# Modulation of the first tiles summed on TensorE in column groups, with TensorE in the program's order

## The chip, the cores and the metric

The kernel runs on one core of a Trainium2 chip. The metric is the device time of one execution in microseconds (us).

## What is computed

Two transformer blocks run one after the other on a sequence of 512 tokens with 1024 features, in float32. The first block has a mixer (a state-space scan beside chunked attention) and a gated feed-forward layer; the second has windowed attention beside an mLSTM, and a mixture of experts. The change touches only the beginning of the first block, where the norm of the input is scaled and shifted by six vectors that a small product of the conditioning vector c gives:

```python
c_act = jax.nn.silu(c)
mod = (c_act @ w_ada[l] + b_ada[l])[:, None, :]
sh_m, sc_m, g_m, sh_f, sc_f, g_f = jnp.split(mod, 6, axis=-1)
h = rmsnorm(x, norm_mix_w[l]) * (1 + sc_m) + sh_m
z, xbc, dt_raw, q, k, v = jnp.split(h @ w_in[l], IN_SPLITS, axis=-1)
```

Only sh_m and sc_m, the first 2048 columns of w_ada, are wanted here; the other four vectors are made later, beside other work.

## The kernel before

Everything is kept transposed: features lie on the 128 partitions, so x is eight tiles xT[:, k, :] of 128 features by 512 tokens. A float32 product is made of three products of a faster type: each operand is split into a high and a low part, and mm3 (lines 273 to 279) issues high x high, low weight x high, high weight x low.

The stage of the change (lines 487 to 574) works off the eight feature tiles k. For each, load(k) fetches 1 MB of w_ada (all 1024 rows for 256 columns: 128 of the shift and 128 of the scale) and 384 KB of w_in. ScalarE makes the high part of the weights (whigh), VectorE the low part (wlow). The 256 modulation values of tile k are sums over 1024 rows, eight blocks of 128: VectorE multiplies the first ND[k] blocks by cact and adds them up (ada0), TensorE adds the rest as products with one column, and a product with ones sums over the partitions (lines 551 and 552). VectorE adds the bias and makes the scale (b, lines 556 and 557), ScalarE applies both to the normed tile xn (h, line 559) and takes its high part hh (line 560), VectorE the low part hl (line 565). Then products(k) adds w0[k] x h into six PSUM tiles (first), eighteen products per tile. The stage begins with the norm: squares on ScalarE, their sum on VectorE (acc), column sums on TensorE (line 361), the root on GpSimd (line 371), and a broadcast by four products with diagonal matrices (lines 380 and 381). Products of zeros (warm, line 244) are issued at the start and once in between.

The order of each engine's instructions is set by a planner at build time, which goes by priority and its own times. Where ip(...) stands, an instruction is held behind the one traced just before it on its engine; most of the stage's VectorE and ScalarE instructions are so held. TensorE's are held by it only in the modulation (lines 551 and 552); the products stand where the planner puts them, and it may put products of the following qk tiles (tile_a, lines 277 to 279 with wh and wl) between them. Tiles of PSUM come from a pool of two (psd) and one of six (psm). The qk tiles take theirs from the pool of two, and so does the first of the six tiles of the stage. The eight DMA loads of xT, four constants, and the loads of w_ada and w_in are issued by the SP queue in this order.

Of the kernel before, what the change touches and what calls it, by code (L numbers as in the profile page):

```python
# [13 lines left out]
AF = mybir.ActivationFunctionType  # L14
ALU = mybir.AluOpType
AX = mybir.AxisListType
PSUM = bass.MemoryType.PSUM
P = 128
EPS = 1e-6
NW0, NW1 = 16, 14  # L20
WAIT = 6
NEG = -1e30

# [159 lines left out]
def _prog(ctx, tc, nc, I, out):  # L183
    PE, DVE, ACT, POOL, SP = nc.tensor, nc.vector, nc.scalar, nc.gpsimd, nc.sync
    pers = ctx.enter_context(tc.tile_pool(name="pers", bufs=1))
# [3 lines left out]
    sm = dense.enter_context(tc.tile_pool(name="sm", bufs=2, side="right", reuse_waits="tile"))  # L189
# [10 lines left out]
    def pt(pool, shape, tag, dt=F32, bufs=None):  # L200
        kw = {} if bufs is None else {"bufs": bufs}
        return pool.tile(shape, dt, tag=tag, name=nm(tag), **kw)
# [8 lines left out]
    def psd():  # L211
        return pt(pd, [P, 512], "d")

    def psm():
        return pt(pm, [P, 512], "m")

    def const(name, shape, pool=pers):
        t = pt(pool, shape, name)
        SP.dma_start(t, I[name])
        return t  # L220
# [4 lines left out]
    HB = hbs.enter_context(tc.tile_pool(name="hb", bufs=1))  # L225
# [4 lines left out]
    xps = ExitStack()  # L230
    XP = xps.enter_context(tc.tile_pool(name="xp", bufs=1, reuse_waits="tile"))
    xT = pt(XP, [P, 8, 512], "xT")
    for k in range(8):
        SP.dma_start(xT[:, k, :], I["xT"][:, k, :])
    ident, tri, strict, ones = (const(n, [P, P], p) for n, p in (("k_ident", pers), ("k_tri", HB), ("k_strict", HB), ("k_ones", sm)))


    zeros = pt(XP, [P, 256], "zeros")
# [2 lines left out]
    def warm(n, zeros=zeros):  # L241
        ps = psm()
        for _ in range(n):
            PE.matmul(ps[:, :256], lhsT=zeros[:, :P], rhs=zeros, start=True, stop=True)
# [8 lines left out]
    def col(name, j=0, n=1):  # L253
        o, _ = _COLS[name]
        if kept:
            return kept[0][:, o - _COLS["final_norm_w"][0] + j :][:, :n]
        return cols[:, o + j : o + j + n]
# [17 lines left out]
    def mm3(ps, w, x, first, last):  # L275
        (wh, wl), (xh, xl) = w, x
        PE.matmul(ps, lhsT=wh, rhs=xh, start=first, stop=False)  # L277
        PE.matmul(ps, lhsT=wl, rhs=xh, start=False, stop=False)  # L278
        PE.matmul(ps, lhsT=wh, rhs=xl, start=False, stop=last)  # L279
# [104 lines left out]
    def norm_cols(n, *parts, ts=range(4), pool=sm):  # L384
        ms = pt(pool, [P, 4], "ms")[:, : len(ts)]
        DVE.tensor_scalar(ms, colsum(*parts, ts=ts, pool=pool), 1.0 / n, EPS, op0=ALU.mult, op1=ALU.add)
        return rstd(ms, pool)
# [36 lines left out]
    cact = pt(pers, [P, 8], "cact")  # L424
# [42 lines left out]
    with xps:  # L467

        hh = pt(HB, [P, 8, 512], "hh", F32R)
        hl = pt(HB, [P, 8, 512], "hl", F32R)  # L470
        def norm_split(oh, ol, x, R, g, ks, hs=slice(0, 512)):
            for k in ks:
                t = pt(XW, [P, 512], "nt")[:, hs]
                DVE.tensor_tensor(t, x[:, k, hs], R, op=ALU.mult)
                ACT.activation(oh[:, k, hs], t, AF.Copy, scale=g[:, k : k + 1])  # L475
                DVE.scalar_tensor_tensor(ol[:, k, hs], t, g[:, k : k + 1], oh[:, k, hs].bitcast(F32), op0=ALU.mult, op1=ALU.subtract)

        def mod_norm(R, s, b, hh, hl, hs):
            for k in range(8):
                t = pt(XW, [P, 512], "nt")[:, hs]  # L480
                DVE.tensor_tensor(t, xT[:, k, hs], R, op=ALU.mult)
                h = pt(XW, [P, 512], "nh")[:, hs]
# [1 line left out]
                split(hh[:, k, hs], hl[:, k, hs], h)  # L484


        with tc.tile_pool(name="ada", bufs=1, reuse_waits="tile") as AD:
            acc = pt(sm, [P, 512], "acc", bufs=1)
            for k in range(8):
                sq = acc if k == 0 else pt(AD, [P, 512], "sq", bufs=3)  # L490
                ACT.activation(sq, xT[:, k, :], AF.Square)
                if k:
                    DVE.tensor_tensor(acc, acc, sq, op=ALU.add)
            first = [psd()] + [psm() for _ in range(5)]
            ip = tc.keep_in_program_order
            wbuf = [pt(HB, [P, 4096], n) for n in ("bh", "bl")]
            wa, w0, whs, wls, xns, accs = [], [], [], [], [], []

            def load(k):
                if k < 8:  # L500
                    wa.append(wbuf[k % 4 // 2][:, 2048 * (k % 2) : 2048 * (k % 2) + 2048])
                    SP.dma_start(wa[k], I["w_ada0"][k])
                    w0.append(pt(AD, [P, 768], "w0", bufs=3))
                    SP.dma_start(w0[k], I["w_x0"][k])

            def ada0(k, a, b):

                if k < 8:
                    if a == 0:
                        accs.append(pt(AD, [P, 256], "acc", bufs=3))  # L510
                        ip(DVE.tensor_scalar(accs[k], wa[k][:, :256], cact[:, 0:1], None, op0=ALU.mult))
                    for i in range(max(a, 1), b):
                        ip(DVE.scalar_tensor_tensor(accs[k], wa[k][:, 256 * i : 256 * i + 256], cact[:, i : i + 1], accs[k], op0=ALU.mult, op1=ALU.add))

            def whigh(k):
                if k < 8:
                    whs.append(pt(AD, [P, 768], "w0h", F32R, bufs=3))
                    ip(ACT.activation(whs[k], w0[k], AF.Copy))

            def wlow(k):  # L520
                if k < 8:
                    wls.append(pt(AD, [P, 768], "w0l", F32R, bufs=3))
                    ip(DVE.tensor_tensor(wls[k], w0[k], whs[k].bitcast(F32), op=ALU.subtract))

            def xnorm(k):
                if k < 8:
                    xns.append(pt(AD, [P, 512], "xn", bufs=3))
                    ip(DVE.tensor_tensor(xns[k], xT[:, k, :], R, op=ALU.mult))

            ND = (5, 5, 6, 7, 6, 6, 7, 6)  # L530
            load(0)
            load(1)
            r = norm_cols(1024, acc)
            warm(4)
            whigh(0)
            ada0(0, 0, 3)
            R = rowbc(r)
            ada0(0, 3, ND[0])
            xnorm(0)
            Rs = pt(AD, [P, 512], "R")  # L540
            ACT.activation(Rs, R, AF.Copy)
            R = Rs
            whigh(1)

            def modulated(k):
                load(k + 2)
                ps = psm()
                for j in range(2):
                    for i in range(ND[k], 8):
                        o = 256 * i + j * P  # L550
                        ip(PE.matmul(ps[:, j : j + 1], lhsT=wa[k][:, o : o + P], rhs=cact[:, i : i + 1], start=(i == ND[k]), stop=False))
                    ip(PE.matmul(ps[:, j : j + 1], lhsT=accs[k][:, j * P : (j + 1) * P], rhs=ones[:, 0:1], start=False, stop=True))
                n = 3 if k else ND[1]
                ada0(k + 1, 0, n)
                b = pt(AD, [P, 3], "b", bufs=2)
                ip(DVE.tensor_tensor(b[:, :2], ps[:, :2], col("b_ada", k, 9)[:, ::8], op=ALU.add))
                ip(DVE.scalar_tensor_tensor(b[:, 2:], b[:, 1:2], 1.0, col("norm_mix_w", k), op0=ALU.add, op1=ALU.mult))
                h = pt(XW, [P, 512], "nh")
                ip(ACT.activation(h, xns[k], AF.Identity, bias=b[:, 0:1], scale=b[:, 2:]))
                ip(ACT.activation(hh[:, k, :], h, AF.Copy))  # L560
                ada0(k + 1, n, ND[min(k + 1, 7)])
                if k == 0:
                    wlow(0)
                wlow(k + 1)
                ip(DVE.tensor_tensor(hl[:, k, :], h, hh[:, k, :].bitcast(F32), op=ALU.subtract))
                xnorm(k + 1)
                whigh(k + 2)

            def products(k, *_):
                w = whs[k], wls[k]  # L570
                for m, o in enumerate(first):
                    mm3(o, [t[:, m * P : (m + 1) * P] for t in w], (hh[:, k, :], hl[:, k, :]), k == 0, k == 7)

            _pipelined([(k,) for k in range(8)], modulated, products)


        y, w_out = _mix1(locals())
# [48 lines left out]
        with tc.tile_pool(name="ffn", bufs=2, reuse_waits="tile") as FF:  # L626
            x = (hh, hl)
            for part, (a, b) in enumerate(_PARTS):
                ah = pt(HB, [P, 8, 512], "hh", F32R)
                al = pt(HB, [P, 8, 512], "hl", F32R)  # L630
                for m in range(a, b):
                    y = []
                    for j in range(2):
                        ps = ups.pop(0) if ups else tile_a(I["w_up"][2 * m + j], x)
                        o = pt(FF, [P, 512], "cv%d" % j)
# [11 lines left out]
                for m in range(8 if part < 2 else 5):  # L647
                    ps = tile_a(dn(m), (ah, al), kt=b - a)
# [64 lines left out]
    o, _ = _COLS["final_norm_w"]  # L713
# [39 lines left out]
    ip = tc.keep_in_program_order  # L753
# [44 lines left out]
def _pipelined(steps, *parts):  # L798

    steps = [list(s) for s in steps]  # L800
    for t in range(len(steps) + len(parts) - 1):
        for j, f in enumerate(parts):
            if 0 <= t - j < len(steps):
                steps[t - j].append(f(*steps[t - j]))
# [907 lines left out]
```

## Time and profile before

| | |
|---|---|
| time, median of 3 runs | 1591.37 us (1588.38 to 1591.61) |
| profiled execution | 1588.89 us, of which span 1587.1 us |
| mean granted TensorE clock | 0.992 |
| TensorE products busy | 1550.4 us, 98% |
| VectorE busy | 850.4 us, 54% |
| ScalarE busy | 524.4 us, 33% |
| HBM read | 315.41 MB |

Times within the span are counted from its start. A busy share over the whole span says little here, since the stage of the change is the first 75 us; it has to be read by windows and by the timeline. In the rows PE is TensorE's products, PEld its weight loads, DVE is VectorE, ACT ScalarE, SPq the queue of SP. Names such as d and m are tiles of the two PSUM pools, w0h and w0l the two parts of the stage's weights, wh and wl those of the qk tiles. A float32 product counts as two instructions, one of the split type as one.

### The profile page before, as it was taken

What the parts mean: (1) busy time and instruction counts of PE and PEld (TensorE: products, weight loads), DVE (VectorE), ACT (ScalarE), POOL (GpSimd) and SP (SyncE); (2) the same over time, 40 slices, a digit from 0 to 9 for tenths busy, and PEclk for the clock granted to TensorE, in tenths of its full rate; (3) what the DMA queues carried; (4) which work ended last, traced back from release to release, by engine and by line L of the source; (5) the groups of instructions that cost most, each with busy time, mean ns of one, the idle gap of its engine ahead of it and who ended that gap; (6) DMA issues with size and microseconds to landing.
All of it is one profiled execution on the core that took longest, in us unless ns stands there. A gap on an engine that the chain in (4) does not pass through costs nothing.

```text
span 1587.1 us, 21111 instructions
## 1 busy us (share of the span) xinstructions
PE 1550.4 (98%) x8208; PEld 1106.1 (70%) x8208; DVE 850.4 (54%) x1679; ACT 524.4 (33%) x964; POOL 35.8 (2%) x33
## 2 busy tenths in 40 slices
PE   8999999999999999989999999999999999999997
PEld 7878857988888888978976688866535545545443
DVE  7777886674564466668467724454242332332333
ACT  4453375442442344443456722231101101101101
POOL 0002000000000000000101000000000000000000
PEclk8999999999999999999999999999999999999999
DMA  8365423333233234402201023497999999999992
GB/s 331 135 197 175 167 73 101 126 100 106 100 94 104 95 93 128 145 18 98 89 27 57 29 86 98 141 316 271 392 369 418 418 415 418 419 417 417 418 417 75
DMA packets 92598, 321.02 MB, mean 202 GB/s; under 512 B 10412, under 2 KB 13100, under 8 KB 91472
## 3 DMA queue, kind: packets, MB, share of 16 engines
q1 hardware_dynamic: 92496, 319.64, 54.1%
q8 instruction: 66, 1.08, 0.3%
q14 instruction: 36, 0.29, 0.1%
HBM read 315.41 MB, written 4.19 MB: 201 GB/s over the span
## 4 chain that ended last, share of the span: by engine, by line
PE 90%; DVE 5%; ACT 2%; DMA 1%; issue 1%; POOL 1%; SPq 0%; DVEq 0%; ACTq 0%
PE d L1522 21%; PE d L277 15%; PE d L278 15%; PE d L279 15%; PE m L1508 4%; PE m L1624 4%; PE m L277 1%; PE m L279 1%; PE m L278 1%; PE m L1219 1%; PE m L1204 1%; DMA wr<-w_ada 1%; PE m L1039 1%; POOL rstd L371 1%; ACT S L1317 1%
## 5 line engine op out<-in xcount | busy, mean ns | idle before, releaser
L1522 PE MATMUL d<-we,xg 128*64 128x512 f32 x1024 | 226.6, 595 | 0.0
L261 DVE TENSOR_TENSOR wl<-wr,wh 128x1024 fp32r<-128x1024 f32 (+1 forms) x148 | 178.1, 1206 | 79.7 <-ACT wh L260 79.1
L277 PE MATMUL d<-bh,wh 128*128 128x512 f32 (+1 forms) x544 | 210.3, 387 | 2.6 <-ACT bh L475 1.5
L279 PE MATMUL d<-bl,wh 128*128 128x512 f32 (+1 forms) x544 | 209.7, 385 | 0.0
L278 PE MATMUL d<-bh,wl 128*128 128x512 f32 (+1 forms) x544 | 209.6, 385 | 0.0
L260 ACT ACTIVATE wh<-wr 128x1024 fp32r<-128x1024 f32 (+1 forms) x148 | 154.0, 1044 | 147.5 <-PE d L279 120.2
L1522 PEld LDWEIGHTS d<-we,xg 128*64 128x64 f32 x1024 | 70.8, 137 | 134.4 <-issue 121.6
L277 PE MATMUL d<-hh,wh 128*128 128x512 f32 (+1 forms) x392 | 147.2, 376 | 0.7 <-ACT bh L845 0.7
L278 PE MATMUL d<-hh,wl 128*128 128x512 f32 (+1 forms) x392 | 145.9, 373 | 0.0
L279 PE MATMUL d<-hl,wh 128*128 128x512 f32 (+1 forms) x392 | 145.8, 373 | 0.0
L277 PEld LDWEIGHTS d<-bh,wh 128*128 128x128 f32 x544 | 102.4, 188 | 25.0 <-issue 2.2
L278 PEld LDWEIGHTS d<-bh,wl 128*128 128x128 f32 x544 | 102.4, 188 | 22.2 <-issue 2.6
L279 PEld LDWEIGHTS d<-bl,wh 128*128 128x128 f32 x544 | 102.6, 189 | 20.1 <-issue 0.5
L1522 PE MATMUL d<-we,aT 128*64 128x512 f32 x512 | 112.6, 592 | 0.7 <-ACT aT L1597 0.7
L1522 PEld LDWEIGHTS d<-we,aT 128*64 128x64 f32 x512 | 36.7, 137 | 73.5 <-issue 71.4
L1625 DVE TENSOR_TENSOR xt<-xt,m 128x512 f32<-128x512 f32 x120 | 73.8, 681 | 22.8 <-PE m L1624 22.8
L277 PEld LDWEIGHTS d<-hh,wh 128*128 128x128 f32 x392 | 73.8, 188 | 16.8 <-issue 2.3
L1608 ACT ACTIVATE yh<-d,ws 128x512 fp32r<-128x512 f32 x32 | 22.0, 688 | 185.2 <-PE d L1522 185.2
L279 PEld LDWEIGHTS d<-hl,wh 128*128 128x128 f32 x392 | 73.7, 188 | 13.7 <-issue 0.5
L278 PEld LDWEIGHTS d<-hh,wl 128*128 128x128 f32 x392 | 73.9, 188 | 12.5
L638 DVE SCALAR_TENSOR_TENSOR cv<-d,cols,cv 128x511 f32<-128x511 f32 x41 | 30.7, 749 | 77.3 <-ACT cv L637 77.3
L1597 ACT ACTIVATE aT<-m 128x512 f32<-128x512 f32 x16 | 9.6, 598 | 176.5 <-PE m L1595 176.5
(430 smaller groups left out, 2631.6 us busy)
## 6 DMA issues: line engine op xcount, KB each, us to landing
we<-w_eg SPq DMA_DIRECT2D x128, 512.0 KB, 9.9
we<-w_eu SPq DMA_DIRECT2D x128, 512.0 KB, 8.9
we<-w_ed SPq DMA_DIRECT2D x128, 512.0 KB, 9.9
wr<-w_up SPq DMA_DIRECT2D x44, 512.0 KB, 3.3
wr<-w_ada SPq DMA_DIRECT2D x32, 512.0 KB, 4.0
wr<-w_out SPq DMA_DIRECT2D x16, 512.0 KB, 3.5
wr<-w_dn SPq DMA_DIRECT2D x16, 512.0 KB, 3.6
wr<-w_mg SPq DMA_DIRECT2D x16, 512.0 KB, 3.3
```

The lines of the kernel that those rows point to most:

```text
L260: ACT.activation(hi, src, AF.Copy)
L261: DVE.tensor_tensor(lo, src, hi.bitcast(F32), op=ALU.subtract)
L277: PE.matmul(ps, lhsT=wh, rhs=xh, start=first, stop=False)
L278: PE.matmul(ps, lhsT=wl, rhs=xh, start=False, stop=False)
L279: PE.matmul(ps, lhsT=wh, rhs=xl, start=False, stop=last)
L371: POOL.tensor_tensor(r, ms, mhalf.to_broadcast((P, n)), op=ALU.pow)
L638: DVE.scalar_tensor_tensor(o[:, 1:], ps[:, :511], wc(1), o[:, 1:], op0=ALU.mult, op1=ALU.add)
L1508: PE.matmul(ps[:, :n], lhsT=hx[:, T, d * P : (d + 1) * P], rhs=oh[:, T, :n], start=(T == 0 and hx is hth), stop=(T == 3 and hx is htl))
L1522: PE.matmul(ps[x * m : (x + 1) * m], lhsT=xs[x][:, k, :], rhs=w[k // 2][x][:, k % 2 * 512 : k % 2 * 512 + 512], start=(k == 0), stop=(k == ...
L1608: ACT.activation(yh[:, s], ps, AF.Copy, scale=ws)
L1624: PE.matmul(ps, lhsT=oht[:, T * P : (T + 1) * P], rhs=y[:, s], start=(i == 0), stop=(i == len(mm) - 1))
L1625: DVE.tensor_tensor(xt[:, T, s], xt[:, T, s] if len(done) > 1 else hth[:, T, s].bitcast(F32), ps, op=ALU.add)
```

## The change

VectorE's sums (ada0) and the one-column products are removed. Instead cact is laid out in a zeroed tile cz, 32 columns for each of the eight row blocks, of which the first holds the values. modulation(k) multiplies block i by the 256 columns of w_ada, in the column group i % 4 of 32 output partitions; the blocks i and i + 4 share a group. Each group then holds one row of partial sums and 31 of zeros. ScalarE copies the 128 x 256 result to SBUF (part), and columns(k) sums it over the partitions with two products with ones; b follows as before. modulation(k + 2) and whigh(k + 2) stand in the middle of products(k), columns(k + 1) ahead of products(k), and modulation(0) ahead of the norm's column sums. TensorE issues the whole block in the program's order. Besides, the opening products of zeros are 21 in place of 16, those in between 3 in place of 4, xT is loaded by four DMAs in place of eight, and two constants are loaded behind the first two tiles' weights.

```diff
-NW0, NW1 = 16, 14
+NW0, NW1, NW2 = 21, 14, 3
...
-    for k in range(8):
-        SP.dma_start(xT[:, k, :], I["xT"][:, k, :])
-    ident, tri, strict, ones = (const(n, [P, P], p) for n, p in (("k_ident", pers), ("k_tri", HB), ("k_strict", HB), ("k_ones", sm)))
+    for k in range(0, 8, 2):
+        SP.dma_start(xT[:, k : k + 2, :], I["xT"][:, k : k + 2, :])
+    ident, ones = (const(n, [P, P], p) for n, p in (("k_ident", pers), ("k_ones", sm)))
...
-        with tc.tile_pool(name="ada", bufs=1, reuse_waits="tile") as AD:
+        with tc.tile_pool(name="ada", bufs=1, reuse_waits="tile") as AD, tc.manual_schedule(engines={mybir.EngineType.PE}):
...
-            first = [psd()] + [psm() for _ in range(5)]
...
+            cz = pt(AD, [P, 8, 32], "cz")
+            DVE.memset(cz, 0.0)
+            DVE.tensor_copy(cz[:, :, 0], cact)
...
-            def ada0(k, a, b):
-
-                if k < 8:
-                    if a == 0:
-                        accs.append(pt(AD, [P, 256], "acc", bufs=3))
-                        ip(DVE.tensor_scalar(accs[k], wa[k][:, :256], cact[:, 0:1], None, op0=ALU.mult))
-                    for i in range(max(a, 1), b):
-                        ip(DVE.scalar_tensor_tensor(accs[k], wa[k][:, 256 * i : 256 * i + 256], cact[:, i : i + 1], accs[k], op0=ALU.mult, op1=ALU.add))
...
+            def modulation(k):
+
+                if k >= 8:
+                    return
+                ps = psm() if k % 2 else psd()
+                for i in range(8):
+                    g = 32 * (i % 4)
+                    PE.matmul(ps[g : g + 32, :256], lhsT=cz[:, i, :], rhs=wa[k][:, 256 * i : 256 * i + 256], start=(i < 4), stop=(i >= 4))
+                part = pt(AD, [P, 256], "acc", bufs=2)
+                mps.append((ps, part))
+                ip(ACT.activation(part, ps[:, :256], AF.Copy))
+
+            def columns(k):
+                if k >= 8:
+                    return
+                ps, part = mps[k]
+                for j in range(2):
+                    PE.matmul(ps[:, 256 + j : 257 + j], lhsT=part[:, j * P : (j + 1) * P], rhs=ones[:, 0:1], start=True, stop=True)
+                b = pt(AD, [P, 3], "b", bufs=3)
+                ip(DVE.tensor_tensor(b[:, :2], ps[:, 256:258], col("b_ada", k, 9)[:, ::8], op=ALU.add))
+                ip(DVE.scalar_tensor_tensor(b[:, 2:], b[:, 1:2], 1.0, col("norm_mix_w", k), op0=ALU.add, op1=ALU.mult))
+                bs.append(b)
+
             load(0)
             load(1)
+            tri, strict = (const(n, [P, P], HB) for n in ("k_tri", "k_strict"))
+            modulation(0)
             r = norm_cols(1024, acc)
-            warm(4)
+            columns(0)
+            warm(NW2)
             whigh(0)
-            ada0(0, 0, 3)
             R = rowbc(r)
-            ada0(0, 3, ND[0])
+            wlow(0)
             xnorm(0)
             Rs = pt(AD, [P, 512], "R")
             ACT.activation(Rs, R, AF.Copy)
             R = Rs
+            modulation(1)
             whigh(1)
+            first = [psd()] + [psm() for _ in range(5)]
...
             def modulated(k):
                 load(k + 2)
...
+                b = bs[k]
                 h = pt(XW, [P, 512], "nh")
                 ip(ACT.activation(h, xns[k], AF.Identity, bias=b[:, 0:1], scale=b[:, 2:]))
                 ip(ACT.activation(hh[:, k, :], h, AF.Copy))
-                ada0(k + 1, n, ND[min(k + 1, 7)])
-                if k == 0:
-                    wlow(0)
+                columns(k + 1)
                 wlow(k + 1)
                 ip(DVE.tensor_tensor(hl[:, k, :], h, hh[:, k, :].bitcast(F32), op=ALU.subtract))
                 xnorm(k + 1)
-                whigh(k + 2)
...
-            def products(k, *_):
+            def products(k):
                 w = whs[k], wls[k]
                 for m, o in enumerate(first):
                     mm3(o, [t[:, m * P : (m + 1) * P] for t in w], (hh[:, k, :], hl[:, k, :]), k == 0, k == 7)
+                    if m == 2:
+                        modulation(k + 2)
+                        whigh(k + 2)
...
-            _pipelined([(k,) for k in range(8)], modulated, products)
+            for k in range(8):
+                modulated(k)
+                products(k)
```

## Rows read from the trace of the kernel before

**Rows 1.** The page: the chain that ended last, its shares by engine.
```profile
PE 90%; DVE 5%; ACT 2%; DMA 1%; issue 1%; POOL 1%; SPq 0%; DVEq 0%; ACTq 0%
```

**Rows 2.** Windows: length, busy us (instructions) of PE, PEld, DVE, ACT, POOL; clock, DMA, GB/s.
```profile
30.00:35.00 5.00, 5.00 (x30) 4.32 (x29) 4.72 (x12) 2.29 (x3) 0.00 (x0) 1.00 0.94 358
```

**Rows 3.** Timeline of TensorE in the stage: start us, us, engine, line, operation, operands.
```profile
24.14 0.77 PE L277 MATMUL d<-hh,w0h 128*128 128x512 f32 x1
...
31.43 0.48 PE L277 MATMUL d<-hh,w0h 128*128 128x512 f32 x1
...
33.13 0.40 PE L279 MATMUL d<-hl,w0h 128*128 128x512 f32 x1
...
51.82 0.48 PE L277 MATMUL d<-hh,w0h 128*128 128x512 f32 x1
...
56.75 0.40 PE L277 MATMUL d<-hh,wh 128*128 128x512 f32 x1
...
70.55 0.40 PE L277 MATMUL d<-hh,wh 128*128 128x512 f32 x1
...
72.77 0.50 PE L277 MATMUL d<-hh,wh 128*128 128x512 f32 x1 [0.69 <-ACT bh L845]
```

**Rows 4.** Chain in order of time, 94 to 99 us, around narrow(): start us, us.
```profile
94.82 3.57 PE d L298 x32
98.39 0.43 PE d L277
98.82 0.23 PE d L278
```

**Rows 5.** Chain in order of time: two pieces of the one-column products.
```profile
46.37 0.34 PE m L551 x4
46.93 0.45 PE m L551 x4
```

**Rows 6.** Timeline of VectorE and ScalarE in one tile.
```profile
31.60 0.16 DVE L556 TENSOR_TENSOR b<-m,cols 128x2 f32<-128x2 f32 x1
31.80 0.16 DVE L557 SCALAR_TENSOR_TENSOR b<-b,cols 128x1 f32<-128x1 f32 x1
...
31.99 0.81 ACT L559 ACTIVATE nh<-xn,b 128x512 f32<-128x512 f32 x1 [0.78 <-DVE b L557]
...
32.84 0.63 ACT L560 ACTIVATE hh<-nh 128x512 fp32r<-128x512 f32 x1
...
33.83 0.95 DVE L523 TENSOR_TENSOR w0l<-w,w0h 128x768 fp32r<-128x768 f32 x1
...
34.70 0.68 DVE L565 TENSOR_TENSOR hl<-nh,hh 128x512 fp32r<-128x512 f32 x1
...
35.87 0.85 ACT L518 ACTIVATE w0h<-w 128x768 fp32r<-128x768 f32 x1 [2.39 <-PE m L279]
```

**Rows 7.** Timeline of the start.
```profile
1.22 8.60 PE L244 MATMUL m<-zeros 128*128 128x256 f32 x32 [1.22 <-DVE zeros L239]
...
9.10 0.33 SPq L502 DMA_DIRECT2D bh<-w_ada  x1
...
13.38 1.05 PE L361 MATMUL m<-k_ones,acc 128*128 128x1 f32 x8 [3.56 <-DVE acc L493]
...
15.76 0.88 DVE L380 TENSOR_SCALAR diag<-k_ident,rstd 128x128 f32<-128x128 f32 x4 [1.13 <-POOL rstd L371]
...
17.78 1.06 PE L381 MATMUL m<-diag,k_ones 128*128 128x128 f32 x8
```

**Rows 8.** Waits of TensorE: us in total, times, longest.
```profile
PE d L279 <- DVE wl L261: 2.7, 1, 2.7
```

**Rows 9.** DMA issues between 8 and 10 us: KB each, us to landing.
```profile
bh<-w_ada SPq DMA_DIRECT2D x1, 1024.0 KB, 5.4
```

**Rows 10.** Windows of TensorE alone: length, busy (instructions), clock, DMA, GB/s.
```profile
662.90:666.30 3.40, 2.54 (x23) 1.00 0.67 230
666.30:669.70 3.40, 3.40 (x18) 0.50 0.40 140
```

More of the change, by code (lines that the diff above doesn't have):

```diff
@@ L493, in _prog @@
                     DVE.tensor_tensor(acc, acc, sq, op=ALU.add)
-            first = [psd()] + [psm() for _ in range(5)]
             ip = tc.keep_in_program_order
             wbuf = [pt(HB, [P, 4096], n) for n in ("bh", "bl")]
-            wa, w0, whs, wls, xns, accs = [], [], [], [], [], []
+            wa, w0, whs, wls, xns = [], [], [], [], []
+            cz = pt(AD, [P, 8, 32], "cz")
+            DVE.memset(cz, 0.0)
+            DVE.tensor_copy(cz[:, :, 0], cact)
             def load(k):
@@ L528, in xnorm @@
                     ip(DVE.tensor_tensor(xns[k], xT[:, k, :], R, op=ALU.mult))
-            ND = (5, 5, 6, 7, 6, 6, 7, 6)
+            bs, mps = [], []
+            def modulation(k):
[18 more added lines that the diff above has]
+                bs.append(b)
             load(0)
             load(1)
+            tri, strict = (const(n, [P, P], HB) for n in ("k_tri", "k_strict"))
+            modulation(0)
             r = norm_cols(1024, acc)
-            warm(4)
+            columns(0)
+            warm(NW2)
             whigh(0)
-            ada0(0, 0, 3)
             R = rowbc(r)
-            ada0(0, 3, ND[0])
+            wlow(0)
             xnorm(0)
@@ L542, in _prog @@
             R = Rs
+            modulation(1)
             whigh(1)
+            first = [psd()] + [psm() for _ in range(5)]
             def modulated(k):
                 load(k + 2)
[L547 to L557, printed above, removed]
+                b = bs[k]
                 h = pt(XW, [P, 512], "nh")
```

## The prediction

> **What bounds the kernel now.** I read the page's shares of the chain first: TensorE carries 90% of what ended last [rows 1], so a stage costs what TensorE spends in it, waits included. The table by windows comes next: between 30 and 35 us, inside the stage that is rewritten, TensorE is busy 5.00 of 5 us and VectorE 4.72 [rows 2]; both are full, so relieving VectorE alone frees nothing unless TensorE also has less to do. Then TensorE's timeline [rows 3]. The stage's first product starts at 24.14. Tile 5 (I call the eight contraction blocks k tiles) starts at 51.82, products of the first qk tile come in between from 56.75, and from 70.55 the rest of that qk tile follows. The second qk tile starts at 72.77, after 0.69 us of waiting for a PSUM buffer. That start is my mark: all behind it is untouched code, so the change is worth what it does to these 72.77 us.
>
> **What is removed.** VectorE loses five to seven operations per tile (ada0). TensorE loses the one-column products of modulated(): pieces of four cost 0.34 to 0.45 us on the chain [rows 5], so the 12 to 16 instructions of most tiles cost 1.0 to 1.6 us, and they lay on TensorE's path.
>
> **What modulation(k) costs.** Eight products in four column groups are 16 instructions of 256 columns. The nearest rows are those of narrow(), the same form at 512 columns: 32 instructions in 3.57 us [rows 4], so half the count at half the width is 3.57 / 4 = 0.89 us if the groups overlap as there. The first full-width product behind it took 0.43 in place of 0.23 [rows 4], so going back costs 0.20; with the entry I take 1.2. The lower bound is 0.9; the upper, without overlap, is 16 x 0.27 = 4.3 by the opening warming products of the same width (8.60 us for 32) [rows 7]. I stay near the narrow rows. columns(k) is four one-column instructions, 0.34 to 0.45 [rows 5]; I take 0.5 with the switch.
>
> **What the order costs, the term that decides.** TensorE now keeps the program's order: products(k-1), columns(k+1), products(k). VectorE's order is pinned too: the two b operations behind columns(k+1), then wlow(k+1), then hl(k), then xnorm. And hl(k) is an operand of the third product of tile k. So when TensorE leaves tile k-1, the third product of tile k is away by columns 0.5, the b pair 0.36 (31.60 to 31.96), wlow 0.87 from its start to that of hl, hl 0.68 [rows 6] and two hand-overs of some 0.03 (b ends 31.96, nh starts 31.99 [rows 6]): 2.5 us. TensorE has columns and two products to do in that time, 0.5 + 2 x 0.23 = 0.96, and waits 1.5 us. Queued behind that third product are all sixteen others of the tile and modulation(k+2), with ScalarE's part copy and whigh behind those. Before, hl(k) came late on VectorE as well, but the planner had put the high products of several column blocks ahead of the first low one: in tile 1 that one starts at 33.13, 1.7 us behind the tile's first at 31.43, and nothing waits [rows 3]. The other loop is not late: part (about 0.4, from 0.85 for 768 columns and 0.63 for 512), whigh 0.85, nh 0.81 and hh 0.63 [rows 6] make 2.7 us, and TensorE has half of products(k), 2.1 us, and the 0.5 of columns from modulation's end to the next tile: hh is some 0.1 to 0.2 us behind the wait that is there anyway.
>
> A tile 1 to 5 therefore costs 2.5 + 16 x 0.23 + 1.2 = 7.4 us. Before, 24.14 to 51.82 is 27.7 us for five tiles, 5.5 each, with the slow clock of the first ones in it [rows 3].
>
> On whether a waiting product lets others pass, the trace has one product of line 279 that waited 2.7 us for VectorE [rows 8]; what was ready behind it no row says. The Trainium skill, "TensorE: Matmul & The Clock Gate", Part 3 (the mechanism), says that weight loads may be pulled ahead but products start and end strictly in order. By that the wait stands as summed; were products passed, the sum would be the TensorE-bound one of the second rival below.
>
> **The start.** The ada tensor of tile 0 is issued at 9.10 and lands 5.4 us later [rows 7, 9], at 14.5. The change moves two constants of 64 KB behind it, worth about 0.3 us at the 358 GB/s of [rows 2], so 14.2; xT in pairs moves the same bytes. In TensorE's order modulation(0) now stands ahead of the column sums of the norm, which began at 13.38 [rows 7]. They begin at 14.2 + 1.0 = 15.2. From there to the fourth diag took 15.76 + 0.88 - 13.38 = 3.3 us [rows 7], giving 18.5; columns(0) and six warming instructions (0.5 + 6 x 0.27 = 2.1) end behind the 1.05 of the sums at about 18.4, so they are hidden; at half clock, where the same columns take twice the time, they would end about 1 us later. Row broadcast ends near 18.8, as before (17.78 + 1.06 = 18.84 [rows 7]). Then, in ScalarE's pinned order, modulation(1) 1.1, part 0.45, whigh 0.75, nh 0.84, hh 0.63: the first product stands at about 22.6 and, with hl behind it, the third at 23.5. At half clock add 1 us. The five extra opening warming products lie in time in which TensorE was idle.
>
> **The sum.** Third product of tile 0 at 23.5; tile 0 ends at 23.5 + 3.7 + 1.2 = 28.4. Five tiles at 7.4 give 65.4. Tile 6 has no modulation: 2.5 + 3.7, so 71.6. Tile 7 has no columns behind which hl could stand: 18 x 0.23 = 4.1, so 75.7. The 24 products of the first qk tile, done partly inside the stage before, follow: 5.5, so 81.2. No wait for a PSUM buffer is left then, since the first tile's has had 5.5 us to be emptied. Against 72.77 that is 8.5 us later. One credit: the planner may still put products of the qk tile into a wait of the stage. They need a buffer of the pool of two, of which one is held by first and the other by the even modulations until columns(6), and split qk weights, which came late before. I credit the wait of tile 6, 1.5 us: +7.0 us.
>
> The profiled execution took 1588.89 us (span 1587.1 and 1.8 around it), so it would be 1595.9; the median of the three runs is 2.5 above it, so the forecast is 1591.4 + 7.0 = 1598.4. Its own range, from two waits filled (+5.5) to none and a half-clock start (+10), is 1597 to 1601.5; the later stages, planned anew, I cannot price and allow 1.5 either way, half the spread of the runs.
>
> **Rivals.** First, the waits are filled: if the buffer and the split weights are there early enough for the whole first qk tile (5.5 us) to go into four waits of 1.5, the mark moves by 8.5 - 5.5 = +3.0: 1594.4. For it: the planner did this once before [rows 3]. Against: the buffer, and that no such product stands inside tiles 0 to 4 before. Chance 0.17.
>
> Second, not slower: hl(k) is there in time and TensorE alone bounds the stage. Then 22.6 + 144 x 0.23 + 6 x 1.2 + 6 x 0.5 + 5.5 = 71.4, or 1.3 us earlier than the mark: 1590.1. It decides at the wait of the third product: under 0.6 us per tile the sum of 8.5 falls by 6 x 0.9 and is within what I can call unchanged. For it: VectorE keeps only 0.36 + 0.95 + 0.68 [rows 6] and an xnorm as long as hl, 2.7 us, per tile. Against: the pinned order, in which nothing that VectorE saves comes ahead of columns(k+1). Chance 0.15.
>
> Third, the waits cost clock too. From 666.3 to 669.7 the granted clock was 0.50, 1.2 in place of 2.4 GHz, and in the stretch ahead of it TensorE had been idle for 0.9 us [rows 10]. Around each new wait lie 1.5 us of idle time and 0.5 of one-column products. Three such stretches, each with 1 to 1.7 us of product time lost, add 4: 1602.4. Chance 0.12.
>
> Fourth, the change does not do what it says: the groups don't overlap. 6 x (4.3 - 1.2) in the tiles and 2 x 3.1 at the start add 25: about 1623. Chance 0.03; narrow() speaks against it.
>
> **How the numbers follow.** The forecast has 0.53. 0.2% is 3.2 us, about what a measurement of this kernel tells from none. Of the second rival I put 0.07 on faster by more than that (a cheaper modulation, an earlier start) and 0.08 within; of the first 0.09 within and 0.08 above. So faster 0.07, within 0.17, slower 0.76. The range from 1590 to 1604 leaves out the lower part of the second rival and the upper parts of the third and fourth.
>
> **What would show it.** In the profile after: 32 tile-group instructions of two modulations in about 1.9 us; TensorE waiting some 1.5 us for hl on VectorE, about six times, at line 279's counterpart in mm3; the first product near 22.6, tile starts 7.4 apart, the second qk tile's start near 80. A tile spacing under 6.2, or qk products inside tiles 1 to 4, would make the forecast wrong; so would hl ahead of wlow on VectorE.

## The result and the profile after

| | before | after |
|---|---|---|
| time, median | 1591.09 us (1588.38 to 1591.61, 4 runs) | 1601.57 us (1598.84 to 1602.97, 4 runs) |
| profiled execution | 1588.89 us, span 1587.1 | 1601.70 us, span 1599.6 |
| second qk tile starts (the prediction's mark) | 72.77 us | 84.41 us |
| narrow() starts | 94.75 us | 106.39 us |
| TensorE clock, mean | 0.992 | 0.993 |

The changed kernel is slower: the ratio is 1.0068, with a 95% interval from 1.0052 to 1.0084, or 10.5 us between the medians. The prediction was 1598.4 us and a range from 1590 to 1604.

The page of the kernel after has TensorE at a smaller share of the chain that ended last, against the 90% of [rows 1]; its busy times stand in the second line.

```profile
PE 88%; DVE 5%; ACT 2%; DMA 2%; issue 1%; POOL 1%; SPq 0%; DVEq 0%; ACTq 0%
...
PE 1557.0 (97%) x8280; PEld 1101.6 (69%) x8280; DVE 830.3 (52%) x1633; ACT 525.4 (33%) x972; POOL 35.6 (2%) x33
```

VectorE was relieved by 20 us of work (850.4 to 830.3), and the kernel is 10.5 us longer. The window from 30 to 35 us, with all engines, answers [rows 2]. Its columns are the same.

```profile
30.00:35.00 5.00, 3.70 (x18) 2.11 (x21) 2.40 (x5) 0.00 (x0) 0.00 (x0) 0.81 0.53 184
```

VectorE falls from 4.72 to 2.40, as intended, but TensorE falls from 5.00 to 3.70 at a clock of 0.81: it waits where it had been full. What it waits for stands in the table of waits of TensorE from 24 to 85 us (us in total, times, longest):

```profile
PE d L279 <- DVE hl L575: 5.3, 4, 1.4
PE d L277 <- ACT hh L572: 1.5, 1, 1.5
PE d L277 <- ACT bh L859: 0.7, 1, 0.7
PE d L277 <- DVE b L545: 0.3, 1, 0.3
```

The first row is the wait that the prediction named. The timeline shows how it comes about; here is tile 3, first on TensorE, then on ScalarE and VectorE (the rows answer [rows 3] and [rows 6]).

```profile
45.91 0.40 PE L279 MATMUL m<-hl,w0h 128*128 128x512 f32 x1
46.14 0.50 PE L543 MATMUL d<-k_ones,acc 128*128 128x1 f32 x4
46.60 0.51 PE L277 MATMUL d<-hh,w0h 128*128 128x512 f32 x1
46.94 0.39 PE L278 MATMUL d<-hh,w0l 128*128 128x512 f32 x1
48.64 0.50 PE L279 MATMUL d<-hl,w0h 128*128 128x512 f32 x1 [1.30 <-DVE hl L575]
48.97 0.40 PE L277 MATMUL m<-hh,w0h 128*128 128x512 f32 x1
...
50.47 1.07 PE L533 MATMUL m<-bh,cz 128*32 128x256 f32 x16
51.47 0.50 PE L277 MATMUL m<-hh,w0h 128*128 128x512 f32 x1
51.81 0.40 PE L278 MATMUL m<-hh,w0l 128*128 128x512 f32 x1
...
54.15 0.51 PE L277 MATMUL d<-hh,w0h 128*128 128x512 f32 x1
```

```profile
45.92 0.63 ACT L572 ACTIVATE hh<-nh 128x512 fp32r<-128x512 f32 x1
...
46.74 0.16 DVE L545 TENSOR_TENSOR b<-d,cols 128x2 f32<-128x2 f32 x1 [5.10 <-PE d L543]
46.94 0.16 DVE L546 SCALAR_TENSOR_TENSOR b<-b,cols 128x1 f32<-128x1 f32 x1
47.02 0.96 DVE L517 TENSOR_TENSOR w0l<-w,w0h 128x768 fp32r<-128x768 f32 x1
47.90 0.69 DVE L575 TENSOR_TENSOR hl<-nh,hh 128x512 fp32r<-128x512 f32 x1
```

VectorE stands idle for 5.10 us until columns(4), L543, is done on TensorE. Only then do b, wlow(4) and hl(3) follow, one behind the other, and TensorE, which has two products to do in that time, waits 1.30 us. What hl(3) itself needs is there earlier: ScalarE ends hh(3) at 46.55, and hl(3) starts at 47.90. From columns(4) at 46.14 to the third product at 48.64 it is 2.50 us. The tile takes 54.15 - 46.60 = 7.55 us.

The second thing is the clock, read from the windows of TensorE alone (length, busy, clock, DMA, GB/s):

```profile
30.00:33.20 3.20, 1.90 (x8) 0.98 0.23 44
33.20:36.60 3.40, 3.40 (x21) 0.52 0.97 395
36.60:57.10 20.50, 16.52 (x95) 1.00 0.59 209
57.10:60.40 3.30, 3.30 (x21) 0.50 0.44 128
```

Two stretches inside the stage run at the lower of the two levels, 1.2 in place of 2.4 GHz, each about 1 us behind the end of a wait for hl (waits that end at 32.03 and 56.18). The tiles with such a stretch take longer: tile 1, from 29.99 to 38.98, takes 8.99 us. Two waits of the same kind, in tiles 2 and 3, have no such stretch behind them.

### The profile page after: what moved, and what is told of

It is laid out like the page before. It is cut to its first block, busy times and chain, and to the rows that moved or that the text cites. A ratio compares the mean times of both kernels' runs of the same rounds, so it can differ in the third digit from the quotient of the medians.

```text
span 1599.6 us, 21219 instructions
## 1 busy us (share of the span) xinstructions
PE 1557.0 (97%) x8280; PEld 1101.6 (69%) x8280; DVE 830.3 (52%) x1633; ACT 525.4 (33%) x972; POOL 35.6 (2%) x33
## 4 chain that ended last, share of the span: by engine, by line
PE 88%; DVE 5%; ACT 2%; DMA 2%; issue 1%; POOL 1%; SPq 0%; DVEq 0%; ACTq 0%
PE d L1536 21%; PE d L277 15%; PE d L279 15%; PE d L278 14%; PE m L1522 4%; PE m L1638 4%; PE m L277 1%; PE m L279 1%; PE m L278 1%; PE m L1233 1%; PE m L1218 1%; PE m L1053 1%; ACT S L1331 1%; POOL rstd L371 1%; PE m L1016 1%
## 5 line engine op out<-in xcount | busy, mean ns | idle before, releaser
L278 PEld LDWEIGHTS d<-bh,wl 128*128 128x128 f32 x544 | 102.6, 189 | 23.6 <-issue 2.6
```

## The experiments

The theory is that the wait for hl makes the loss, through the order: hl(k) is pinned behind work that begins only when TensorE has left tile k-1. Its rivals are the clock (half-clock stretches make the loss, and the waits only bring them), the modulation itself (column groups cost more than what they replace), the start (the opening products, the loads, the constants), and TensorE's fixed order as such. The times, with the start of narrow() as the mark common to all, and the distance of two neighbouring tiles at full clock in the profiled execution. One execution of each kernel is profiled, and the half-clock stretches ahead of tile 1 differ between kernels with the same opening code. So the medians are compared, and the marks only with these stretches in view:

| kernel | median us | ratio to before, 95% | narrow() starts | tile |
|---|---|---|---|---|
| after | 1601.57 | 1.0068 [1.0052, 1.0084] | 106.39 | 7.55 |
| hl first on VectorE | 1592.86 | 1.0023 [1.0003, 1.0043] | 97.14 | 6.23 |
| high products first | 1589.99 | 0.9989 [0.9980, 0.9999] | 94.78 | 5.84 |
| TensorE to the planner | 1599.99 | 1.0055 [1.0038, 1.0072] | 103.66 | 6.81 |
| wlow twice | 1612.43 | 1.0140 [1.0123, 1.0157] | 118.53 | 10.1 (not at full clock) |
| start alone | 1590.38 | 0.9992 [0.9983, 1.0001] | 94.60 | |
| zeros in the waits | 1600.33 | 1.0052 [1.0033, 1.0072] | 105.99 | 7.55 |
| modulation one tile further ahead | 1589.44 | 0.9990 [0.9981, 1.0000] | 93.76 | 5.85 |
| modulation in three pieces | 1597.93 | 1.0053 [1.0036, 1.0069] | 102.83 | 6.92 |
| high products first, no second zeros | 1591.33 | 1.0006 [0.9997, 1.0016] | 97.55 | 5.84 |

### hl first on VectorE

The order of VectorE alone is changed: hl(k), whose operands are ScalarE's, is traced ahead of columns(k+1), b and wlow(k+1).

```diff
+                ip(DVE.tensor_tensor(hl[:, k, :], h, hh[:, k, :].bitcast(F32), op=ALU.subtract))
                 columns(k + 1)
                 wlow(k + 1)
-                ip(DVE.tensor_tensor(hl[:, k, :], h, hh[:, k, :].bitcast(F32), op=ALU.subtract))
```

> Edit: hl(k) is traced ahead of columns(k+1), so on VectorE it no longer stands behind the b pair and wlow(k+1); TensorE's order is unchanged. Theory (the wait for hl behind columns on VectorE is what costs): the waits of 1.30 to 1.37 us on the third product shrink to about 0.3, since hl still follows hh (0.63 + 0.16 + 0.69); five tiles give about -5 us, and up to 3 more if the two stretches at half clock inside the stage go with them: 1593 to 1597. Rival (TensorE's added modulation work and its switches are what costs): waits move elsewhere, the time stays within 2 us of the changed kernel, 1600 to 1603. Rival (the slow clock alone): the time falls only if the half-clock stretches go, and then by some 3 us.

It took 1592.86 us, 8.7 less than the changed kernel, just below what the theory expected. Its six times spread from 1591.15 to 1598.66, and all lie below the four of the changed kernel (1598.84 and more); the profiled one is among the short ones, 1592.23. The waits of TensorE between 24 and 80 us, and the window of all engines over that time:

```profile
PE d L277 <- ACT hh L572: 0.8, 1, 0.8
PE d L279 <- DVE hl L573: 0.6, 1, 0.6
```

```profile
24.00:80.00 56.00, 54.63 (x306) 39.43 (x305) 26.72 (x48) 24.57 (x38) 0.00 (x0) 1.00 0.46 167
```

One wait for hl of 0.6 us is left of four with 5.3 us, and no half-clock stretch in the stage: the clock is 1.00. The same instructions in the stage, with one operation moved, give back 8.7 of 10.5 us. So neither the modulation in groups nor TensorE's fixed order as such makes most of the loss; the place of hl does, with the half clock that went with it.

### High products first

VectorE's order stays that of the changed kernel; TensorE's products are put so that the late operand is wanted late.

```diff
                 for m, o in enumerate(first):
-                    mm3(o, [t[:, m * P : (m + 1) * P] for t in w], (hh[:, k, :], hl[:, k, :]), k == 0, k == 7)
-                    if m == 2:
+                    for i in range(2):
+                        PE.matmul(o, lhsT=w[i][:, m * P : (m + 1) * P], rhs=hh[:, k, :], start=(k + i == 0), stop=False)
+                    if m == 3:
                         modulation(k + 2)
                         whigh(k + 2)
+                for m, o in enumerate(first):
+                    PE.matmul(o, lhsT=w[0][:, m * P : (m + 1) * P], rhs=hl[:, k, :], start=False, stop=(k == 7))
```

> Edit: VectorE's order stays as in the change; TensorE issues the twelve products of a tile that need no hl first, modulation(k+2) behind the eighth of them, and the six that need hl last. Theory: 1.5 us of wait are covered by 2.3 us of products, so no product waits for hl in tiles 1 to 6; tile spacing 5.8 in place of 7.5; second qk tile starts near 74 to 75 in place of 84.4: 1591 to 1593. Rival (TensorE's added work): spacing stays near 7, time within 3 us of the changed kernel.

It took 1589.99 us, a little less than expected. Over the same window TensorE is busy throughout:

```profile
24.00:80.00 56.00, 56.00 (x315) 41.45 (x314) 28.09 (x49) 26.13 (x40) 0.00 (x0) 0.97 0.48 177
```

Its tiles start at 29.72, 35.56, 41.40 and 47.25, 5.84 us apart.

```profile
29.72 0.48 PE L582 MATMUL d<-hh,w0h 128*128 128x512 f32 x1
...
35.56 0.48 PE L582 MATMUL d<-hh,w0h 128*128 128x512 f32 x1
```

This answers the question that the rows of before left open, whether products behind a waiting product may pass it. The ten high products of the other column blocks have only hh, w0h and w0l as operands; here they run in the time until hl is there, and in the changed kernel, with the same operands ready, none of them starts in the 1.30 us. The Trainium skill, "TensorE: Matmul & The Clock Gate", Part 3 (the mechanism), has products start and end strictly in order; the two traces agree.

### TensorE to the planner

```diff
-        with tc.tile_pool(name="ada", bufs=1, reuse_waits="tile") as AD, tc.manual_schedule(engines={mybir.EngineType.PE}):
+        with tc.tile_pool(name="ada", bufs=1, reuse_waits="tile") as AD:
```

> Edit: the change without the fixed order on TensorE, which is left to the planner as before the change. Theory: the planner moves products that need no hl ahead of those that wait, as it did before the change, so the waits for hl go, and the time is near that of high products first, 1591 to 1594. Rival (the column-group work itself is what costs): still 1598 or more.

This missed: it took 1599.99 us, nearly as long as the changed kernel, though the wait for hl is gone. The planner did put high products ahead, as before the change, but it also cut the modulations of the later tiles into pieces (those of tiles 0 to 2 are whole, that of tile 3 is in two pieces, the others in three). TensorE in one tile:

```profile
39.60 0.63 PE L533 MATMUL d<-bh,cz 128*32 128x256 f32 x6
40.16 0.50 PE L277 MATMUL d<-hh,w0h 128*128 128x512 f32 x1
...
41.76 0.62 PE L533 MATMUL d<-bh,cz 128*32 128x256 f32 x4
...
43.21 0.63 PE L533 MATMUL d<-bh,cz 128*32 128x256 f32 x6
43.77 0.50 PE L277 MATMUL m<-hh,w0h 128*128 128x512 f32 x1
```

The tile, to the next one's start at 46.97, costs 46.97 - 40.16 = 6.81 us, TensorE without a wait. Either the cuts or the half clock of its start (23.2 to 30.0 us) could make the loss of this kernel; the pieces by hand, below, tell them apart.

### wlow twice

The disputed wait is lengthened by one more operation of 0.95 us, the same wlow written again, ahead of hl.

```diff
                 wlow(k + 1)
+                if k < 7:
+                    ip(DVE.tensor_tensor(wls[k + 1], w0[k + 1], whs[k + 1].bitcast(F32), op=ALU.subtract))
                 ip(DVE.tensor_tensor(hl[:, k, :], h, hh[:, k, :].bitcast(F32), op=ALU.subtract))
```

> Edit: in the changed kernel wlow(k+1) is written twice, so that hl(k) stands behind one more VectorE operation of 0.9 us; VectorE has 5 us of idle time per tile for it. Theory: the wait of the third product grows by 0.88 us in tiles 1 to 4, and by up to as much in tiles 5 and 6, where products of the qk tile fill a part: +3.5 to +5.5 us on the changed kernel, 1605 to 1607. Rival (hl is not on the path): no change, 1601.6.

The direction was right and the size not: 1612.43 us, 10.9 more than the changed kernel. Of its five waits for hl one is 0.28 us, and the four others, 2.28 to 2.59, are longer than the 1.30 by about the 0.95 us that was added or a little more; behind each of these four comes a half-clock stretch. First the waits, then one of them in the timeline with what follows, then the windows:

```profile
PE d L279 <- DVE hl L577: 9.9, 5, 2.6
```

```profile
46.62 0.51 PE L279 MATMUL d<-hl,w0h 128*128 128x512 f32 x1 [2.28 <-DVE hl L577]
...
49.12 1.94 PE L533 MATMUL d<-bh,cz 128*32 128x256 f32 x16
```

```profile
37.30:40.70 3.40, 3.40 (x21) 0.51 0.95 388
47.60:50.90 3.30, 3.30 (x20) 0.50 0.99 406
57.80:61.10 3.30, 3.30 (x21) 0.50 1.02 346
68.00:71.30 3.30, 3.22 (x7) 0.51 0.54 176
```

Tiles 1 to 3 start 10.1 us apart, 2.55 more than 7.55: about 1 of it is the longer wait, and 1.5 is a clock stretch that each of the four tiles has now. That is the same 1.5 as in tile 1 of the changed kernel (8.99 - 7.55 = 1.44). So the wait decides, and what a wait costs is more than its length. Not all of the 12.1 us by which narrow() starts later than in the changed kernel is from these tiles: tile 1 starts at 33.51 in place of 29.99, since tile 0 lay in a half-clock stretch here, from 23.6 to 30.6 us, that began ahead of any wait for hl. From the column sums ahead of tile 1 to those behind tile 4 it is 8.3 us more.

### Zeros in the waits

Six products of zeros with 128 columns (twelve instructions) go into the wait of tiles 1 to 4, into an unused part of a PSUM tile. The waits stay as long; TensorE isn't idle in them.

```diff
...
+                    if m == 0 and 0 < k < 5:
+                        for _ in range(6):
+                            PE.matmul(mps[k + 1][0][:, 384:512], lhsT=zeros[:, :P], rhs=zeros[:, :P], start=True, stop=True)
...
```

> Edit: in tiles 1 to 4 of the changed kernel six products of zeros (128 columns, 0.21 us each at full clock) stand between the second and the third product, that is in the wait for hl; the wait itself keeps its length. This separates the two ways in which a wait costs. Theory: four waits of 1.3 us remain and only the half-clock stretches that follow them go (two in the profiled run of the changed kernel, about 1.5 us each): 1597.5 to 1600, with no half-clock stretch between 25 and 65 us. Rival (the slow clock is most of the loss): 1595 or less. Rival (the clock plays no part): 1601 to 1603.

It took 1600.33 us, 1.2 less than the changed kernel and just above what the theory expected. Four executions each, 1596.48 to 1603.58 here, don't tell the two apart: by the time alone it is not shown that the clock plays a part, only that it isn't most of the loss. One wait, and the windows of TensorE:

```profile
48.33 1.50 PE L586 MATMUL d<-zeros 128*128 128x128 f32 x12
49.79 0.50 PE L587 MATMUL d<-hl,w0h 128*128 128x512 f32 x1
```

```profile
23.20:30.00 6.80, 6.01 (x26) 0.50 0.96 392
32.00:62.00 30.00, 30.00 (x201) 1.00 0.59 209
```

With the waits filled by zeros the clock is 1.00 from 32 to 62 us, where the changed kernel had 0.52 and 0.50 in two stretches; the tiles start at 32.66, 40.21, 47.76 and 55.30, 7.55 apart. So in these two executions the half clock between 32 and 62 us came with idle time only, and at full clock throughout the tiles, with the same delay of the third product, are as long as the unslowed ones of the changed kernel. In the profiled execution, 1601.95 us, nothing of the clock's part came back in the total: tile 0 ran at half clock in it, which it did not in the profiled execution of the changed kernel.

### The start alone

The kernel before, with only the edits of the start: more opening zeros, fewer in between, xT in pairs, two constants later.

```diff
-NW0, NW1 = 16, 14
+NW0, NW1, NW2 = 21, 14, 3
...
-    for k in range(8):
-        SP.dma_start(xT[:, k, :], I["xT"][:, k, :])
+    for k in range(0, 8, 2):
+        SP.dma_start(xT[:, k : k + 2, :], I["xT"][:, k : k + 2, :])
...
```

> Edit: the kernel before with the start's edits alone: 21 opening products of zeros, 3 in between, xT in four loads, two constants loaded behind the first weights; modulation stays on VectorE and TensorE's order is the planner's. Theory: the start is no part of the loss; its effect is that of the clock in the first 30 us, 0 to 2 us gained: 1589 to 1591.5. Rival (the new loading order delays the norm): 1592 to 1594.

1590.38 us, not to be told from before; the first product stands at 24.07 (24.14 before). So these edits have no part in the loss. That modulation(0) stands ahead of the norm's column sums is not among them; but in the changed kernel the first product stands at 23.76, no later than before.

### Modulation in three pieces

High products first, and the eight modulation products cut by hand into 3, 2 and 3, behind the column blocks 0, 1 and 3. The edit is shown against that kernel, as it is in the next two.

```diff
...
-                    if m == 3:
-                        modulation(k + 2)
+                    if m in (0, 1, 3):
+                        modulation(k + 2, *{0: (0, 3), 1: (3, 5), 3: (5, 8)}[m])
+                    if m == 3:
                         whigh(k + 2)
```

> Edit: high products first as in e2, but in the loop each modulation is cut into pieces of three, two and three products with full-width products between them, as the planner cut it in the run without a fixed order. Theory of that run's loss (cut groups overlap less and every piece pays its way in and out): a modulation costs 1.7 us in pieces in place of 1.0, with two more switches of 0.2 to 0.3 each; some 1.0 to 1.2 us per tile in six tiles, 6 us over the run with whole groups: 1595 to 1597. Rival (the loss came from the half clock at the start and a later first product): 1589.5 to 1591.

1597.93 us, 7.9 more than the same kernel with the group in one piece, so a little more than expected. In one tile:

```profile
39.38 0.63 PE L537 MATMUL d<-bh,cz 128*32 128x256 f32 x6
39.94 0.50 PE L588 MATMUL m<-hh,w0h 128*128 128x512 f32 x1
40.28 0.40 PE L588 MATMUL m<-hh,w0l 128*128 128x512 f32 x1
40.60 0.63 PE L537 MATMUL d<-bh,cz 128*32 128x256 f32 x4
41.16 0.50 PE L588 MATMUL m<-hh,w0h 128*128 128x512 f32 x1
```

Each piece holds TensorE 0.56 us (39.38 to 39.94, 40.60 to 41.16), whether it has six instructions or four: a column group gets two of them in either. Three pieces make 1.68 where the whole takes 1.00 (50.47 to 51.47 in the changed kernel). Besides, the step from a full-width product into a piece takes 0.32 and the first product out of it 0.34, in place of 0.23: 0.2 us for each piece. The sum, 3 x 0.76 - 1.2 = 1.08 us, is the measured distance of the tiles, 6.92 against 5.84. That explains most of the miss of the planner's kernel: what it gained by its order it lost by the cuts. Of the 10.0 us by which it is slower than high products first, the cuts by hand make 7.9; how the other 2 arise was not tested. The Trainium skill, "TensorEngine Tiling (Array Packing)", Key Properties, says that a change of the tiling mode drains TensorE; the 0.2 us at the edges of each piece fit that, and the 0.56 for a part-filled piece comes on top.

### High products first, without the second zeros

```diff
-NW0, NW1, NW2 = 21, 14, 3
+NW0, NW1, NW2 = 21, 14, 0
```

> Edit: high products first as in e2, without the three products of zeros between the column sums and the row broadcast. Theory: at full clock they end before the fourth diag is there, so they cost nothing and what they buy is clock; without them the row broadcast is as early or up to 1 us earlier, but the first tiles run at half clock for 3.4 to 6.8 us: 1590 to 1592.5. Rival (they only stand in the way): 1588.5 to 1589.5.

1591.33 us, 1.3 more than with the three zero products. The clock and the first product:

```profile
15.70:29.40 13.70, 11.16 (x58) 0.51 1.02 409
```

```profile
24.13 0.80 PE L582 MATMUL d<-hh,w0h 128*128 128x512 f32 x1 [1.08 <-ACT hh L572]
```

The first product comes at 24.13, where it came at 22.31 with them. With a start at half clock it is 1.8 us later in these two executions.

### Modulation one tile further ahead

The version meant to beat both: high products first, modulation(2) ahead of products(0), and modulation(k+3) and load(k+3) within tile k.

```diff
...
-                load(k + 2)
+                load(k + 3)
...
-                        modulation(k + 2)
+                        modulation(k + 3)
...
+            load(2)
...
+                if k == 0:
+                    modulation(2)
                 products(k)
```

> Edit: high products first, and each modulation one tile earlier, so that modulation(2) lies in the 1.5 us in which TensorE waits for hh of tile 0; part gets three buffers, and loads go one tile further ahead. Theory (the stage is bound by TensorE once no product waits): 1.0 to 1.2 us less work between the first product and the second qk tile, and the 3.4 us at half clock at the stage's start may go with the idle time, 1.5 us more: 1587 to 1589, faster than the kernel before by 0.1 to 0.25%. Rival (the first tiles are bound by the loads): modulation(2) waits for its weights and the gain is nil, 1590.

1589.44 us, just above what was expected. It beats the changed kernel by 12 us; against the kernel before its interval reaches 1.000, so with 0.1% it isn't told from it. Nor is it told from high products first (1589.99) and so from its rival's 1590: modulation(2) did lie in the time ahead of tile 0's first product, but modulation(3) waited 0.4 us for its weights.

## Why the prediction was right, and where its sizes were off

**What bounds the kernel** held. The stage costs what TensorE spends in it, waits included, and relieving VectorE gave nothing by itself. With all waits gone (high products first) the tile takes 5.84 us, which is just what the second rival's sum has, 18 x 0.23 + 1.2 + 0.5, and the kernel took 1589.99 us against that rival's 1590.1. That the two meet within 0.1 us is partly luck: in the profiled execution narrow() starts at 94.78, no earlier than before's 94.75 where the rival has 1.3 us, with a half-clock stretch (23.6 to 27.0) in tile 0.

**What modulation(k) costs** held: 1.00 us for the group and 0.10 at each edge, so 1.2, with columns(k) 0.46 for the predicted 0.5. The measured price lies near the lower bound, and far from the upper. That the price holds for an uncut group only was not thought of; it doesn't touch the changed kernel, whose order keeps the group whole, but it made most of the planner's miss.

**What the order costs** held in mechanism and in size. The 2.5 us from leaving a tile to the third product of the next were measured as 2.50: 0.60 from columns to b, 0.28 from b to wlow, 0.88 to hl, 0.69 for hl and 0.05 to the product, so 0.1 more in the first term and 0.1 less in the second. The wait came to 1.30 to 1.37 us in place of 1.5, because TensorE had 1.20 us to do in that time and not 0.96: the 0.46 for columns and 0.34 and 0.39 for the two products. The last 0.39 is to the product's end; with nothing to wait for, the third would start 0.23 behind the second, so the delay itself is 1.47. The tile took 7.55 at full clock in place of 7.4; the rest is 0.10 at the first product after the wait. Moving hl alone gave back 8.7 us, and wanting it later gave back 11.6, so this step is shown, not only argued.

**The start** was predicted with two values, 22.6 and 1 us more at half clock, and the lower one went into the sum. The first product stood at 23.76, with a half-clock stretch under the warming products: these took 2.79 us where 1.6 were summed. At full clock it stood at 22.31 and 22.60 in two of the experiments. The load came 0.7 us earlier than summed (modulation(0) starts at 13.52), so the way from there to the first product was 1.8 us longer than summed, and not 1.2. Which value comes is not a matter of the change's code: seven kernels here have the same start, and in one profiled execution of each these warming products took 2.63 to 2.79 us three times and 1.54 four times. So this term could be given as a range only; the kernel before, too, had half-clock stretches, from 14.4 to 17.8 and from 21.2 to 28.0 us.

**The sum.** By the forecast's terms the mark is at 81.2 - 1.5 = 79.7; it was at 84.41, 4.7 later. By the starts of columns() and of tile 7 in the timeline: the start is 1.13 of it (tile 0 ends at 29.53, not 28.4). The two half-clock stretches are 3.07. The other excess of the five tiles, 0.14 to 0.32 each, is 0.88, and that of tiles 6 and 7 is 0.26. The wait for a PSUM buffer at the mark was put at nothing, since the buffer would have had 5.5 us to be emptied; it is there with the same 0.69 us as in [rows 3]. Against these 6.03 us, the credit was too small by 1.34: here are the first products of the first qk tile in two waits.

```profile
63.60 0.50 PE L277 MATMUL d<-hh,wh 128*128 128x512 f32 x1 [0.32 <-DVE b L545]
...
64.87 0.40 PE L277 MATMUL d<-hh,w0h 128*128 128x512 f32 x1
...
70.86 0.47 PE L277 MATMUL d<-hh,wh 128*128 128x512 f32 x1
...
84.41 0.50 PE L277 MATMUL d<-hh,wh 128*128 128x512 f32 x1 [0.69 <-ACT bh L859]
```

Six stand in tile 5 and seven in tile 6, 13 of 24, so both of these waits were filled; one was credited. From 81.06, the end of tile 7, the other eleven follow. The first rival (four waits filled) came true by that half.

**Where it was wrong** is the third rival: it was kept as an alternative of 0.12, with three stretches of 1 to 1.7 us. The stretches came on top of the forecast, two of them, 1.5 us each, where the sum puts the clock inside the stage at nothing; this is its largest error. The prediction had a single row for it, one stretch behind 0.9 us of idle time [rows 10]. In the runs 1.3 us of waiting was followed by one in two of four tiles, 2.3 to 2.6 us in four of four, and none came where zeros filled the waits. The measured median lies nearer to this rival's 1602.4 than to the forecast, and 0.07 us above the forecast's own range, 1597 to 1601.5, before the 1.5 us allowed for the later stages. The upper end of that range had been reached by other terms, no wait filled and a start at half clock, which add up to 9.5 and not 10 by the prediction's own figures.

**The rest.** Of the 12.5 us between the two spans 11.6 lie ahead of narrow(); 0.9 lies behind it and its cause stays open. The difference of the medians is smaller, 10.5, because the profiled execution of before lies 2.2 us under its median and that of after on it; the forecast, made from the profile, added 2.5 of this kind to the changed kernel as well. So the profiled execution was missed by 5.8 us (1595.9 against 1601.7) and the median by only 3.2: the sum was further off than the result shows, and the smaller miss is luck.

**What would show it.** The waits for hl (four, where about six were named), the tile distance at full clock and the absence of qk products from tiles 1 to 4 came as written; two modulations took 2.1 us in place of 1.9; the mark was not near 80. One of the things named that would make the forecast wrong, hl ahead of wlow, is the edit that undid most of the loss.

## What to carry to other kernels

When engines are pinned to the program's order, follow each operand of the first instructions of a stage back through its engine's queue: an operation whose operands are there must not stand behind one that still waits for another engine, and its result should not be wanted third when it can be wanted last. Price a wait on TensorE with the clock that follows it, not only by its length. Leave a set of products in column groups in one piece, and compare a planned order with a written one by what it cuts, not only by the waits that it fills.

## What the hardware showed that was not expected

Waits that are short against a tile were followed by a lower clock: behind waits of 1.30 us the granted clock was 0.52 and 0.50 for stretches of 3.4 and 3.3 us in two tiles of four, behind waits of 2.28 to 2.59 us in four of four, and at 1.00 where products of zeros filled the same time. A set of products in column groups took a time that goes with its fullest group, not with its count: four and six instructions, at most two in a group, both held TensorE 0.56 us, and sixteen, four in each group, 1.00. Whether products of the same opening code run at half clock differed between kernels with the same start: 2.63 to 2.79 us for the six warming instructions in three profiled executions, 1.54 in four.
